# Two layers' split weights and four token operands laid out with steps of 2, 4 or 8 elements

## The chip, the cores and the metric

The kernel runs on one core of one Trainium2 chip. It is one program with five engines: TensorE multiplies (in the profile PE, and PEld for its weight loads), VectorE (DVE) and ScalarE (ACT) do elementwise work, GpSimd (POOL) and SyncE (SP) mostly issue transfers. Each engine works through its own queue in order and waits for the others by semaphores. The metric is the time of one execution on the device in microseconds; lower is better.

## The reference

Two layers over 512 tokens of width 1024, all in float32. Layer 0 mixes by dilated window attention, layer 1 by an mLSTM, and each is followed by a SwiGLU feed-forward of hidden width 2816:

```python
def swiglu(xn, w_in, w_out):
    gu = xn @ w_in
    return (jax.nn.silu(gu[..., :D_FF]) * gu[..., D_FF:]) @ w_out

def reference(x, positions, ...):
    h = x
    for i in range(DEPTH):
        j = i // N_MIXERS
        if i % N_MIXERS == 0:
            h = h + dilated_attention_mixer(rms_norm(h, attn_norm[j]), positions,
                                            attn_w_in[j], attn_w_out[j])
        else:
            h = h + mlstm_mixer(rms_norm(h, mlstm_norm[j]), mlstm_w_in[j], ...)
        h = h + swiglu(rms_norm(h, ffn_norm[i]), ffn_w_in[i], ffn_w_out[i])
    return rms_norm(h, final_norm)
```

## The kernel before

*Three matmuls for one.* TensorE multiplies the reduced type fp32r. To keep the precision of float32, every operand is split: ScalarE copies it into an fp32r tile (the high part, L239), VectorE subtracts that from the original into a second one (the low part, L241). A product is then the sum of high times high, high times low and low times high (`SPLITS`, three matmuls into one PSUM tile). A *chunk* is a tile of 128 partitions by 1024 elements of a weight matrix: four blocks of 128 rows (k) by 256 columns. A matmul takes as its weights 128 of those columns (k and a half m of the chunk), loads them into TensorE (PEld) and streams the token operand past them. Which operand lies where is told in elements: `weights_tiles` gives each chunk its high and its low tile, from pools of three buffers, at an offset inside the tile (`PAD`, and the pairs `WIDE`, `NARROW`, `TOKENS`); inside, the 1024 elements lie next to each other.

*Projections.* `project` and the plain part of the feed-forward (`plain`) multiply such chunks with all 512 tokens (`multiply`, L276: matmuls of 512 columns, 24 for each chunk). The names of the chunks say the matrix: awo (attention output), mqk, mo, mwo (the mLSTM's projections and its output), f0j0 to f1j2 (the first two pairs of hidden blocks of each feed-forward).

*Products.* The rest of the feed-forward's first matrix is done in blocks of 256 hidden columns, gate and up together (j = 4, 6, ... 20: nine blocks in each layer), by Winograd's form of Strassen's scheme: seven products of halves in place of eight. `PRODUCTS` lists them with their order: A11 x B11, S1 x T1, S2 x T2, A12 x B21, S3 x T3, S4 x B22, A22 x T4. A stands for chunks of weights, S for their sums and differences, which VectorE makes (`total`), B and T for quarters of the normalized tokens and their sums and differences, split once per layer by `split_tokens` into high and low tiles of 128 x 4 x 256. A product is 24 matmuls of 256 columns (`product`, L1680; 2 m, 4 k, 3 splits). `prepare` splits the weights of the product that comes two places later (`AHEAD` = 2), so that the splits run beside the products:

```python
            def prepare(key):
                made[key] = split(key)
                ...
        for n, (j, i) in enumerate(todo):
            some(1)
            prepare(n + AHEAD)
            ...
            steps_of[i]()
```

On VectorE a block then has seven low parts, four sums of weights, four rows that evacuate PSUM into the hidden tile, and in layer 1 also transposes of the residual (hB, L2363) that are stored by GpSimd's queue. On ScalarE it has seven high parts and five evacuations. The order on all engines is that of the program's text, as a scheduler of the framework lays it out; the waits come from which tile is read and written.

*Token operands.* `split_tokens` makes the high part with ScalarE (L1539) and the low part either with VectorE (L1544) or, for B11, T1 and T4, by a negated copy and an adding transfer. `T2`, `B21`, `T3` and `B22` go by VectorE. In layer 1, as in layer 0, that happens during the last plain chunks and the first products.

Of the kernel before, what the change touches and what calls it, by code (L numbers as in the profile page):

```python
# [11 lines left out]
F32 = mybir.dt.float32  # L12
F32R = mybir.dt.float32r
I32 = mybir.dt.int32
AF = mybir.ActivationFunctionType
ALU = mybir.AluOpType
AX = mybir.AxisListType
P = 128
# [58 lines left out]
def tile_hybrid_dilated_attn_mlstm(  # L77
# [5 lines left out]
    x = x[0]  # L83
# [138 lines left out]
    def run_late(_):  # L222
        while lows:
            with tc.issue_after(last_on(mybir.EngineType.DVE)):
                lows.pop(0)()

    def weights_tiles(name, at=WIDE):
        return [wp.tile([P, 1024 + PAD], F32R, tag="w" + x, name=name + "_" + x[0], bufs=W_BUFS)[:, o:o + 1024]
                for x, o in zip(("hi", "lo"), at)]

    def split_chunk(chunk, at=WIDE):

        raw, n, view, name = chunk
        if spare and next(splits) % (W_BUFS + 1) == W_BUFS:
            hi, lo = [spare[0].tile([P, 1024], F32R, tag="w%s4" % x, name=name + "_" + x[0]) for x in ("hi", "lo")]
        else:
            hi, lo = weights_tiles(name, at)
        with behind_factors():
            nc.scalar.activation(hi[:, :n], raw[:, :n], AF.Copy)  # L239
        def low():  # L240
            nc.vector.tensor_tensor(lo[:, :n], raw[:, :n], hi[:, :n].bitcast(F32), op=ALU.subtract)  # L241
        if late[0]:
            lows.append(low)
        else:
            with behind_scores():
                low()
        return view(hi), view(lo)
# [53 lines left out]
    class Feed:  # L301

        def __init__(self, ready, plan, ahead=2):
            self.ready, self.plan, self.ahead = ready, plan, ahead
# [1202 lines left out]
    def ffn_in(layer, fp, pair, rbc, hook, following, hid, during):  # L1507
# [21 lines left out]
        def op_tile(i, name):  # L1529
            return fp.tile([P, 4, HALF], F32R, tag="op%d" % i, name="f%d%s" % (layer, name))  # L1530


        ops, raw = {}, {}

        def split_tokens(key, by_dma=False):

            i = [b for _, b in PRODUCTS].index(key)
            hi, lo = ops[key] = [op_tile(2 * i + part, key + "hl"[part]) for part in range(2)]
            nc.scalar.activation(hi, raw[key], AF.Copy)  # L1539
            if by_dma:  # L1540
                nc.scalar.activation(lo, hi.bitcast(F32), AF.Copy, scale=-1.0)
                nc.gpsimd.dma_start(lo, raw[key], accum_op=ALU.add)
            else:
                nc.vector.tensor_tensor(lo, raw[key], hi.bitcast(F32), op=ALU.subtract)  # L1544
# [1032 lines left out]
```

## Time and profile before

| | us |
|---|---|
| two runs | 1348.9 and 1350.14 |
| median | 1349.52 |
| the profiled execution, by the clock of the device | 1350.34 |
| its span in the profile, first to last instruction | 1348.6 |

The span is 1.7 us shorter than the time of its own execution, which holds what lies before and after the program. The profile's page gives, by engine, the busy time with its share of the span; the row of forty slices (each digit the busy tenths of a slice of 33.7 us) shows whether that share is spread evenly:

```profile
PE   9999999999999999999999999999999999999997
DVE  7988789799876399888888899898858988997887
ACT  6676577667674255555577464795534555558855
PEclk9999999999999999999999999999999999999999
DMA  9354244555676357334362743324343535447863
```

TensorE is busy from end to end but for the last slice, at the full clock. The products of layer 0 lie between 521.7 and 693.4 us, those of layer 1 between 1062.3 and 1234.0 us, nine blocks of 19.04 us each.

### The profile page before, as it was taken

The page shows a single profiled execution, that of the slowest core. Times are in us where ns is not written, and L with a number is a line of the kernel's source. Part 1 is how long each engine was busy: PE and PEld are TensorE (multiplying, and loading weights), DVE is VectorE, ACT ScalarE, POOL GpSimd, SP SyncE. Part 2 cuts the span into 40 slices and gives each one's busy share as a digit, 9 for nine tenths or more (in the row PEclk, how much of TensorE's full clock was granted, in tenths as well). Part 3 has the DMA queues.
Part 4 walks back from the last instruction along what each step waited for, and adds up shares of the span by engine and source line. Part 5 has one row for each costly group of instructions (what it writes and reads, how often), then busy time and mean ns, then how long its engine had stood idle before and what let it go on. Part 6 is the DMA issues. An engine that isn't in the chain of part 4 may idle for free. (4 is left out here: it accounts for less than half of the span.)

```text
span 1348.6 us, 23346 instructions
## 1 busy us (share of the span) xinstructions
PE 1329.1 (99%) x9100; PEld 1219.9 (90%) x9100; DVE 1131.8 (84%) x1787; ACT 812.8 (60%) x1303; POOL 196.6 (15%) x272
## 2 busy tenths in 40 slices
PE   9999999999999999999999999999999999999997
PEld 7898899999998889999999998898888999999886
DVE  7988789799876399888888899898858988997887
ACT  6676577667674255555577464795534555558855
POOL 3000013141412001000010110122200202112113
PEclk9999999999999999999999999999999999999999
DMA  9354244555676357334362743324343535447863
GB/s 302 129 180 155 80 141 149 164 175 154 185 267 192 128 148 175 107 123 126 125 157 79 172 129 89 100 64 125 95 121 98 130 128 173 141 139 172 190 172 102
DMA packets 141270, 194.90 MB, mean 145 GB/s; under 512 B 9028, under 2 KB 106116, under 8 KB 141160
## 3 DMA queue, kind: packets, MB, share of 16 engines
q1 hardware_dynamic: 120128, 140.73, 33.3%
q0 software_dynamic: 19808, 52.48, 16.1%
q8 instruction: 71, 1.16, 0.4%
q10 hardware_dynamic: 1224, 0.21, 0.1%
q14 instruction: 39, 0.32, 0.1%
HBM read 167.30 MB, written 22.54 MB: 141 GB/s over the span
## 5 line engine op out<-in xcount | busy, mean ns | idle before, releaser
L1803 POOL DMA_DIRECT2D f0S<-in_ffn_w_out_dram x10 | 8.7, 875 | 245.0 <-DVE f0hid L1719 161.8
L2366 POOL DMA_DIRECT2D hD<-hB x32 | 20.7, 654 | 109.4 <-DVE hB L2363 109.2
L1827 POOL DMA_DIRECT2D f1T<-in_ffn_w_out_dram x15 | 17.8, 1186 | 86.1 <-ACT f1T L1830 40.5
L276 PE MATMUL mo<-n_h,mo_k_h 128*128 128x512 f32 x64 | 25.4, 397 | 0.0
L276 PE MATMUL mo<-n_h,mo_k_l 128*128 128x512 f32 x64 | 25.2, 394 | 0.0
L276 PE MATMUL awo<-ao_h,awo_k_h 128*128 128x512 f32 x64 | 25.2, 393 | 0.0
L276 PE MATMUL mo<-n_l,mo_k_h 128*128 128x512 f32 x64 | 25.1, 393 | 0.0
L276 PE MATMUL mwo<-yo_l,mwo_k_h 128*128 128x512 f32 x64 | 25.1, 392 | 0.0
L276 PE MATMUL mqk<-n_h,mqk_k_h 128*128 128x512 f32 x64 | 25.1, 392 | 0.0
L276 PE MATMUL mwo<-yo_h,mwo_k_l 128*128 128x512 f32 x64 | 25.1, 392 | 0.0
L276 PE MATMUL mqk<-n_l,mqk_k_h 128*128 128x512 f32 x64 | 25.1, 392 | 0.0
L276 PE MATMUL f0j<-n_h,f0j_h 128*128 128x512 f32 x64 | 25.0, 391 | 0.0
L276 PE MATMUL f1j<-n_h,f1j_h 128*128 128x512 f32 x64 | 25.0, 391 | 0.0
L276 PE MATMUL mwo<-yo_h,mwo_k_h 128*128 128x512 f32 x64 | 25.0, 391 | 0.0
L276 PE MATMUL mqk<-n_h,mqk_k_l 128*128 128x512 f32 x64 | 25.0, 391 | 0.0
L276 PE MATMUL awo<-ao_h,awo_k_l 128*128 128x512 f32 x64 | 25.0, 391 | 0.0
L276 PE MATMUL awo<-ao_l,awo_k_h 128*128 128x512 f32 x64 | 25.0, 390 | 0.0
L276 PE MATMUL f0j<-n_h,f0j_l 128*128 128x512 f32 x64 | 24.9, 390 | 0.0
L276 PE MATMUL f1j<-n_h,f1j_l 128*128 128x512 f32 x64 | 24.9, 390 | 0.0
L276 PE MATMUL f0j<-n_l,f0j_h 128*128 128x512 f32 x64 | 24.9, 389 | 0.0
L276 PE MATMUL f1j<-n_l,f1j_h 128*128 128x512 f32 x64 | 24.9, 389 | 0.0
L241 DVE TENSOR_TENSOR v1P_l<-v1W,v1P_h 128x1024 fp32r<-128x1024 f32 x14 | 17.1, 1223 | 9.2 <-ACT v1P_h L239 9.1
(2746 smaller groups left out, 5993.4 us busy)
## 6 DMA issues: line engine op xcount, KB each, us to landing
f0j_w<-in_ffn_w_in_dram SPq DMA_DIRECT2D x17, 512.0 KB, 6.0
f1j_w<-in_ffn_w_in_dram SPq DMA_DIRECT2D x17, 512.0 KB, 6.6
f1T<-in_ffn_w_out_dram POOLq DMA_DIRECT2D x15, 512.0 KB, 7.4
f0hid<-in_ffn_w_in_dram SPq DMA_DIRECT2D x9, 512.0 KB, 5.1
f1hid<-in_ffn_w_in_dram SPq DMA_DIRECT2D x9, 512.0 KB, 5.1
v0W<-in_attn_w_in_dram SPq DMA_DIRECT2D x8, 512.0 KB, 8.2
v1W<-in_attn_w_in_dram SPq DMA_DIRECT2D x8, 512.0 KB, 4.3
awo_k_w<-in_attn_w_out_dram SPq DMA_DIRECT2D x8, 512.0 KB, 4.0
```

What stands on the lines that cost most here:

```text
L241: nc.vector.tensor_tensor(lo[:, :n], raw[:, :n], hi[:, :n].bitcast(F32), op=ALU.subtract)
L276: nc.tensor.matmul(acc, whl[a][:, k, m * P:(m + 1) * P], pairs[b][kk], start=(kk == 0 and (a, b) == SPLITS[0]), stop=(kk == nk - 1 and (a, ...
L1803: nc.gpsimd.dma_start(t, src[1][:, ks], accum_op=ALU.add)
L1827: nc.gpsimd.dma_start(view(to), weight_rows(hk * UNITS + u, n), accum_op=ALU.add)
L2366: nc.gpsimd.dma_start(hD[k // 4].rearrange("(b i) x -> i b x", i=R)[:, :, c0:c0 + R], t[R * a_:R * (a_ + 1)])
```

## The change

The split weights and some token operands are laid out so that the elements that one matmul reads lie 2, 4 or 8 elements apart.

- *Wide chunks.* 42 chunks, in the order of `wide_names`: awo3 (2), f0j0, f0j2, f1j0, f1j2 (4 each), mqk0 to mqk3, mo0 to mo3, mwo0 to mwo3 (2 each). `WIDE_STEPS` has a place for each: step 2 for awo3, f0j0, f0j2 and f1j0, step 4 for f1j2, the eight mqk chunks and both of mo0, step 8 for the others; the tile's offset goes through 0, 8, ... 48, the low part's is the same or 8 more.
- *Chunks of the products.* All 126 (nine blocks, seven products, two layers) take a step by their j: step 2 for j = 4, 10, 14; step 4 for j = 6, 16, 20; step 8 for j = 8, 12, 18.
- *How a chunk is laid out.* With step 2 the two halves m of a row block k are interleaved column by column, with step 4 four of the (k, m) are, with step 8 all eight. `Stepped` gives back 128 columns with that step as a matmul's weights. ScalarE and VectorE write the high and the low part with the step (VectorE reads the high part with it too); with step 4 each does so in two instructions of 512 elements, otherwise in one of 1024.
- *Token operands of layer 1.* T2 and B22 are laid out with step 2 and B21 and T3 with step 4; B11, T1 and T4, and all of layer 0, stay as they were. T2 and B22 are split in four pieces of 256 columns on each of the two engines, B21 and T3 in one.
- Chunks split by `split_stepped` don't go through the branches of `split_chunk` for a spare buffer, for late low parts and behind the factors.

No matmul, transfer or sum is added or left out, and the matmuls come in the same order.

```diff
@@ -224,6 +224,43 @@
             with tc.issue_after(last_on(mybir.EngineType.DVE)):
                 lows.pop(0)()
 
+    WIDE_STEPS = [(s, (o, o + d)) for s in (2, 4, 8) for d in (0, 8) for o in range(0, 56, 7 * 8 // 7)]
+    wide_names = (["awo%d_k%d" % (c, k) for k in range(2) for c in range(3, 4)] +
+                  ["f%dj%d_%d%d" % (f, j, a, k) for f in range(2) for j in (0, 2) for k in range(2) for a in range(2)] +
+                  ["m%s%d_k%d" % (x, c, k) for x in ("qk", "o", "wo") for c in range(4) for k in range(2)])
+    NARROW_STEPS = [(2, (16, 48)), (4, (16, 48)), (8, (16, 48)), (2, (0, 0)), (8, (0, 0)), (2, (16, 16)), (4, (16, 16)),
+                    (8, (16, 16)), (4, (0, 32))]
+
+    class Stepped:
+
+        def __init__(self, t, k, step):
+            form = {2: "p (k c m) -> p k m c", 4: "p (k c l m) -> p k l m c", 8: "p (c k m) -> p k m c"}[step]
+            sizes = {2: dict(k=k, m=2), 4: dict(l=2, m=2, c=P), 8: dict(k=k, m=2)}[step]
+            self.step, self.ap = step, t.rearrange(form, **sizes)
+
+        def __getitem__(self, at):
+            _, k, cs = at
+            m = cs.start // P
+            return self.ap[:, k // 2, k % 2, m] if self.step == 4 else self.ap[:, k, m]
+
+        def like(self, t):
+            if self.step == 4:
+                return t.rearrange("p (k l m c) -> p k l m c", l=2, m=2, c=P)
+            return t.rearrange("p (k m c) -> p k m c", m=2, c=P)
+
+    def split_stepped(raw, name, step, at):
+        hi, lo = (Stepped(t, 4, step) for t in weights_tiles(name, at))
+        view = hi.like(raw)
+        parts = [(slice(None), i) for i in range(2)] if step == 4 else [(slice(None),)]
+        for part in parts:
+            nc.scalar.activation(hi.ap[part[0], part[1]] if step == 4 else hi.ap,
+                                 view[part[0], part[1]] if step == 4 else view, AF.Copy)
+        with behind_scores():
+            for part in parts:
+                h_, l_, r_ = (x[:, part[1]] if step == 4 else x for x in (hi.ap, lo.ap, view))
+                nc.vector.tensor_tensor(l_, r_, h_.bitcast(F32), op=ALU.subtract)
+        return hi, lo
+
     def weights_tiles(name, at=WIDE):
         return [wp.tile([P, 1024 + PAD], F32R, tag="w" + x, name=name + "_" + x[0], bufs=W_BUFS)[:, o:o + 1024]
                 for x, o in zip(("hi", "lo"), at)]
@@ -231,6 +268,11 @@
     def split_chunk(chunk, at=WIDE):
 
         raw, n, view, name = chunk
+        if name in wide_names:
+            return split_stepped(raw, name, *WIDE_STEPS[wide_names.index(name) % len(WIDE_STEPS)])
+        if at is NARROW and name[0] == "f" and name[1:3] in ("0j", "1j"):
+            j = int("".join(c for c in name[3:5] if c.isdigit()))
+            return split_stepped(raw, name, *NARROW_STEPS[(j - 4) // 2])
         if spare and next(splits) % (W_BUFS + 1) == W_BUFS:
             hi, lo = [spare[0].tile([P, 1024], F32R, tag="w%s4" % x, name=name + "_" + x[0]) for x in ("hi", "lo")]
         else:
@@ -1532,10 +1574,29 @@
 
         ops, raw = {}, {}
 
+        class Turned:
+
+            def __init__(self, t):
+                self.t = t
+
+            def __getitem__(self, at):
+                return self.t[:, at[1] // 2, at[1] % 2]
+
         def split_tokens(key, by_dma=False):
 
             i = [b for _, b in PRODUCTS].index(key)
             hi, lo = ops[key] = [op_tile(2 * i + part, key + "hl"[part]) for part in range(2)]
+            step = {"T2": 2, "B21": 4, "T3": 4, "B22": 2}.get(key) if layer else None
+            if step:
+                hi, lo = ops[key] = [t.rearrange("p k n -> p (k n)").rearrange(
+                    "p (k n l) -> p k l n" if step == 2 else "p (k n l) -> p (k l) n", k=4 // step, l=step) for t in (hi, lo)]
+                if step == 2:
+                    for k in range(4):
+                        nc.scalar.activation(hi[:, k // 2, k % 2], raw[key][:, k], AF.Copy)
+                        nc.vector.tensor_tensor(lo[:, k // 2, k % 2], raw[key][:, k], hi[:, k // 2, k % 2].bitcast(F32),
+                                                op=ALU.subtract)
+                    ops[key] = [Turned(t) for t in (hi, lo)]
+                    return
             nc.scalar.activation(hi, raw[key], AF.Copy)
             if by_dma:
                 nc.scalar.activation(lo, hi.bitcast(F32), AF.Copy, scale=-1.0)
```

Two places show what it does to the order. The first is VectorE's queue in layer 1 where the weights of block j = 6 are split beside the products of j = 4 (names with A, or hid and w, are chunks and the places where they were loaded, S the sums, h and l high and low). Before:

```order
L241 TENSOR_TENSOR f1j6A_l<-f1hid_11556,f1j6A_h 128x1024
L1686 TENSOR_TENSOR f1j4g_11594<-f1j_p_11434,f1j4u_11489 128x512
L241 TENSOR_TENSOR f1j6S_l<-f1j6S,f1j6S_h 128x1024
L1719 TENSOR_TENSOR f1hid_11593<-f1j4v_11459,f1j4g_11594 128x2x256
L1651 TENSOR_TENSOR f1j6S<-f1j6S,f1hid_11556 128x1024
```

After:

```order
L261 TENSOR_TENSOR f1j6A_l<-f1hid_11638,f1j6A_h 128x4x128 x2
L1747 TENSOR_TENSOR f1j4g_11678<-f1j_p_11516,f1j4u_11571 128x512
L261 TENSOR_TENSOR f1j6S_l<-f1j6S,f1j6S_h 128x4x128 x2
L1780 TENSOR_TENSOR f1hid_11677<-f1j4v_11541,f1j4g_11678 128x2x256
L1712 TENSOR_TENSOR f1j6S<-f1j6S,f1hid_11638 128x1024
```

Each low part has become two instructions of half the size at the same place; the evacuations (j4g, hid) and the sums stand where they stood. The second place is ScalarE's queue where layer 1's tokens are split, at the end of its plain chunks (f1j_01 and f1j_11). Before:

```order
L1539 ACTIVATE f1B22h<-f1x_11166 128x1024
L1539 ACTIVATE f1B21h<-f1x_11166 128x1024
L239 ACTIVATE f1j_11_h<-f1j_11_w 128x1024
L1539 ACTIVATE f1T1h<-f1t_11317 128x1024
L1539 ACTIVATE f1T3h<-f1x_11165 128x1024
L1541 ACTIVATE f1T1l<-f1T1h 128x1024
L1539 ACTIVATE f1T2h<-f1x_11166 128x1024
```

After:

```order
L1595 ACTIVATE f1B22h<-f1x_11228 128x256
L256 ACTIVATE f1j_01_h<-f1j_01_w 128x4x128 x2
L1595 ACTIVATE f1B22h<-f1x_11228 128x256 x3
L1600 ACTIVATE f1B21h<-f1x_11228 128x4x256
L256 ACTIVATE f1j_11_h<-f1j_11_w 128x4x128 x2
L1600 ACTIVATE f1T1h<-f1t_11387 128x1024
L1600 ACTIVATE f1T3h<-f1x_11227 128x4x256
L1602 ACTIVATE f1T1l<-f1T1h 128x1024
L256 ACTIVATE f1j4A_h<-f1hid_11451 128x4x2x128
L1595 ACTIVATE f1T2h<-f1x_11228 128x256 x4
```

T2 and B22 have come apart into four pieces each, one chunk's high part (f1j_01) now stands after the first piece of B22 instead of ahead of it, and one of block j = 4 stands ahead of T2 instead of behind it.

## The prediction

> **What bounds the kernel now.** I read the page first (busy times), then the chain that ended last, then the stage table of the second feed-forward, then single rows.
>
> ```profile
> PE 1329.1 (99%) x9100; PEld 1219.9 (90%) x9100; DVE 1131.8 (84%) x1787; ACT 812.8 (60%) x1303; POOL 196.6 (15%) x272
> 1081.83 2.72 PE f1j_c L1680 x24
> 1084.55 2.72 PE f1j_p L1680 x24
> ```
>
> The first line is the page's list of busy times, the other two are pieces of the chain. TensorE has almost no gap, and in the products the chain is one product after the other: 24 matmuls of 256 columns in 2.72 us, 113.3 ns each. Seven products make one block of hidden columns (one j): 168 matmuls, 19.04 us. The stage table, with a row for such a block in each layer (after the window and its length: PE, PEld, DVE, ACT, POOL busy, clock, DMA share, GB/s), shows how near the next engine is:
>
> ```profile
> 579.20:598.24 19.04, 19.04 (x170) 19.04 (x169) 16.30 (x17) 9.91 (x12) 0.00 (x0) 1.00 0.36 112
> 1138.79:1157.83 19.04, 19.04 (x170) 19.04 (x169) 17.36 (x19) 9.91 (x12) 4.81 (x8) 1.00 0.56 173
> 1028.00:1062.00 34.00, 34.00 (x151) 28.13 (x151) 29.17 (x39) 18.52 (x20) 2.21 (x2) 1.00 0.59 148
> 815.00:860.00 45.00, 45.00 (x248) 38.76 (x247) 42.54 (x80) 26.52 (x34) 1.66 (x2) 1.00 0.33 94
> ```
>
> VectorE has 2.7 us to spare in a block of layer 0 and 1.7 us in one of layer 1; ScalarE has 9. The clock is full. The weight loads are near their limit too. Where a matmul has only 128 columns, the load sets the pace, and the last output block shows it (start, length):
>
> ```profile
> 1339.84 0.19 PEld L2535 LDWEIGHTS finlast<-f1P_4w_h,f1P 128*128 128x128 f32 x1
> 1339.95 0.19 PEld L2535 LDWEIGHTS finlast<-f1P_4w_l,f1P 128*128 128x128 f32 x1
> 516.90 0.39 PE L276 MATMUL f0j<-n_h,f0j_h 128*128 128x512 f32 x1
> 517.12 0.39 PE L276 MATMUL f0j<-n_l,f0j_h 128*128 128x512 f32 x1
> ```
>
> So a dense load of 128 columns takes 0.11 us. A matmul of 512 columns gives it 0.227 us (the lower rows), one of 256 columns 0.113 us: 3 ns to spare.
>
> **The change part by part.** No matmul, transfer or sum is added; what moves is the address step inside the split weights and four token operands. That touches four readers or writers: VectorE's low parts, ScalarE's high parts, TensorE's weight loads, TensorE's streamed tokens. The trace of before has one store with a step of four elements and two such reads, against rows of the same work without a step:
>
> ```profile
> L2012 DVE TENSOR_TENSOR hn<-fo,h x8: 1098/1124/1153, 782.0 to 803.3; 128x512 f32<-128x512 f32 x8
> L1430 DVE TENSOR_TENSOR hn<-mwo,hn x8: 683/690/692, 983.8 to 1017.6; 128x512 f32<-128x512 f32 x8
> L455 DVE CAST angles<-posi x4: 261/270/289, 2.8 to 3.7; 1x128 f32<-1x128 int32 x4
> L463 DVE SCALAR_TENSOR_TENSOR angles<-angles x3: 291/291/293, 6.7 to 7.4; 128x128 f32<-128x128 f32 x3
> L833 DVE TENSOR_TENSOR a1ex<-a1xps,cst x1: 283/283/283, 277.0 to 277.0; 128x128 f32<-128x128 f32 x1
> ```
>
> The store at L2012 writes every fourth element and takes 1124 ns where the dense one takes 690: 434 ns more on 512 elements, 0.85 ns each. The reads at L455 (SBUF) and L833 (PSUM) step by four and cost no more than the dense 128 at L463. Stores with a step are dear, then; reads are not, at VectorE's pace of about one element per ns.
>
> *Low parts on VectorE* (126 in the products, 42 elsewhere). The dense rows, with ScalarE's, and two of the waits of one block from the timeline:
>
> ```profile
> L241 DVE TENSOR_TENSOR f1j_l<-f1j_w,f1j_h 128x1024 fp32r<-128x1024 f32 x8 | 9.8, 1222 | 1.4 <-ACT f1j_h L239 1.2
> L239 ACT ACTIVATE f1j_h<-f1j_w 128x1024 fp32r<-128x1024 f32 x8 | 8.4, 1054 | 10.4 <-PE f1j L276 9.3 <-PE mwo L276 1.1
> 1131.81 1.23 DVE L241 TENSOR_TENSOR f1j10A_l<-f1j10A,f1j10A_h 128x1024 fp32r<-128x1024 f32 x1 [0.34 <-ACT f1j10A_h L239]
> 1134.53 1.22 DVE L241 TENSOR_TENSOR f1j12A_l<-f1hid,f1j12A_h 128x1024 fp32r<-128x1024 f32 x1 [0.29 <-ACT f1j12A_h L239]
> 1137.25 1.22 DVE L241 TENSOR_TENSOR f1j12S_l<-f1j12S,f1j12S_h 128x1024 fp32r<-128x1024 f32 x1 [0.29 <-ACT f1j12S_h L239]
> ```
>
> Step 8: 1222 + 2 x 434 = 2090, 868 more. Step 4 is two halves of 512: 2 x 1124 = 2248, 1026 more. Step 2 has no row; between 0 and 868 I take 0, since the dense row is nearer to two neighbours in 16 bytes than to none. Of the nine blocks three have step 2, three step 4, three step 8. A step-4 block adds 7 x 1.03 = 7.2 us to VectorE, a step-8 block 7 x 0.87 = 6.1. In layer 0 that is 16.3 + 7.2 = 23.5 and 22.4 against TensorE's 19.04: over by 4.5 and 3.4, in sum 3 x 4.5 + 3 x 3.4 = 23.7 us. The lows run only two products ahead (three buffers), so little of that can be saved up in the step-2 blocks.
>
> *High parts on ScalarE.* No row of ScalarE stores with such a step: between nothing and VectorE's 0.85 ns an element, 0.87 us a chunk. Its sum even then is 9.9 + 6.1 = 16.0 of 19.04, so it is no bound. But VectorE's queue waits for it ahead of three of the seven lows (the rows above), and the later sums and evacuations stand behind. At the high end 3 x 0.87 = 2.6 us a block, 12 blocks, 31 us; at the low end 0. I take half, 16 us.
>
> *Token operands of layer 1.* T2 and B22 stream with step 2, B21 and T3 with step 4: 48 matmuls of each kind in a block, 432 in all. The dense stream takes 0.44 ns an element. VectorE's dense pace is (1222 - 690) / 512 = 1.04 ns an element, and the stepped reads of L455 and L833 fall behind it by nothing, so 256 stepped elements take at most 256 x 1.04 = 266 ns instead of 113, if TensorE reads them no worse than VectorE. Between 1 and 2.35 times I take twice for step 4, near the upper end, since TensorE would have to read more than twice as fast as any stepped read in the trace to lose nothing, and once for step 2, as with the low parts. Cost: 432 x 113.3 = 49.0 us, the ends 0 and 66. In these blocks TensorE then needs 19.04 + 5.44 = 24.5 us, and VectorE 17.36 + 7.2 = 24.6: VectorE's extra time in layer 1 is covered, to 0.1 us a block.
>
> *Weight loads.* Step 4 and 8 read 128 elements in 110 ns, 0.86 ns each, nearly the pace at which L455 and L833 show no penalty. I take 0; the other end is twice 110 (a rival below). Where matmuls have 512 columns even 220 hides under 227.
>
> *Plain chunks and token splits.* Eight mqk chunks add 8.2 us to VectorE where it has 2.5 us to spare in 45; not all of its work there is waited for: 4 us. Ahead of the layer-1 products four step-4 chunks and four token splits add 6.7 us to a window with 4.8 to spare: 2 us. The mo, mwo, awo and step-2 chunks meet a VectorE with room. In sum 6 us, between 0 and 10.
>
> Sum against the profiled execution, 1350.34 us (span 1348.6, 0.8 us above the median of 1349.52): 23.7 + 16 + 49.0 + 6 = 94.7, so **1445 us**.
>
> [...]
>
> **Rivals.**
> - A, *the weight load becomes the bound.* Stepped loads at half pace take 220 ns; it decides from 113 ns on. In 12 blocks 2016 matmuls go from 113.3 to 220: 215 us. The tokens then add only in the three step-2 blocks, 3 x 48 x 113.3 ns = 16 us, and 2 us in the others (227 over 220); VectorE is covered; plus 6: 1350 + 239 = 1589 us. For it: 3 ns of margin. Against it: the free stepped reads.
> - B, *the tokens stream free.* VectorE then bounds both layers: 23.7, and in layer 1 3 x 5.5 + 3 x 4.4 = 29.7, plus 16 and 6: 1426 us.
> - C, *tokens go by lines.* If a 16-byte line costs the stream what four dense elements cost (1.77 ns), step 2 is twice, step 4 four times: 9 x (48 x 113.3 + 48 x 340) ns = 196 us in layer 1, plus 23.7, 8 and 6: 1584 us. With A on top it passes 1700.
> - D, *not slower.* The 434 ns of L2012 are then a matter of its PSUM source read beside the dense one, not of the step, and a stepped low stays under 1222 + 2700 / 7 = 1600 ns: VectorE's spare time holds it, tokens and loads run free: 1350 us. If the step even took the 3 ns of margin out of the products (113.3 to 110 for 3024 matmuls), 10 us went: 1340. Against it: same shape, same operation, 690 with a PSUM source too (L1430).
>
> **How the numbers follow.** My forecast 0.37, A 0.29, B 0.15, C 0.07, D 0.12. The forecast's own range is 1405 (no ScalarE share, tokens at 1.8) to 1480. The range on record reaches from B's low side (half of the ScalarE share gone, 1395) to A with a little above: 1395 to 1605; it leaves out D and the combination beyond A, under 2 in 10. Two per cent, 27 us, is about what a measurement of this kernel tells from no change: below 1322.5 faster 0.03, within 0.09 (D), above 1376.5 slower 0.88.
>
> **What the changed profile would show.** Low parts of 2.1 us at step 8 and twice 1.12 at step 4, 1.22 at step 2; high parts of 1.1 (or 1.9) us; PE waiting for low parts in layer 0's step-4 and step-8 blocks. Layer 1's products on B21 and T3 at 5.4 us, on T2 and B22 at 2.72. Starts of stepped weight loads 0.113 us apart as before: 0.22 is rival A. I am wrong if lows stay under 1.6 us, if loads slow down, or if step 2 already costs.

## The result, and the profile after

The changed kernel takes 1679.55 us (two runs, 1678.90 and 1680.19) against 1349.52: 1.2445 times as long, 95% interval 1.2392 to 1.2499. The forecast was 1445, its range 1395 to 1605. The direction was right, the size was not. The profiled execution has a span of 1677.1 us.

The page's list of busy times after the change:

```profile
PE 1640.6 (98%) x9100; PEld 1552.0 (93%) x9100; DVE 1241.6 (74%) x1849; ACT 939.0 (56%) x1365; POOL 195.2 (12%) x272
```

TensorE is still busy from end to end, with the same 9100 matmuls, 311.5 us more of it. So in the main it does not wait for VectorE's parts, as the forecast had it: its own instructions became slower. Where, the table of stages tells (window and its length, then PE, PEld, DVE, ACT, POOL busy, clock, DMA share, GB/s); layer 0's products, the stretch between the two layers' products, and layer 1's products, before:

```profile
521.66:693.45 171.79, 171.79 (x1514) 171.55 (x1513) 150.00 (x152) 97.17 (x122) 3.90 (x4) 1.00 0.43 129
693.45:1062.30 368.85, 367.19 (x2236) 324.29 (x2235) 311.18 (x618) 218.55 (x388) 45.78 (x64) 1.00 0.43 113
1062.30:1233.99 171.69, 171.69 (x1513) 171.50 (x1512) 154.36 (x160) 96.58 (x122) 30.61 (x44) 1.00 0.47 143
```

and after:

```profile
522.34:822.78 300.44, 300.44 (x1514) 300.44 (x1512) 190.03 (x172) 143.43 (x143) 5.67 (x6) 1.00 0.26 77
822.78:1225.95 403.17, 386.38 (x2235) 368.23 (x2235) 336.64 (x634) 248.31 (x404) 43.27 (x62) 0.98 0.38 99
1225.95:1562.95 337.00, 334.27 (x1513) 329.47 (x1512) 199.15 (x185) 146.79 (x148) 30.91 (x45) 0.99 0.26 77
```

The 328.5 us of span are 128.7 in layer 0's products, 34.3 between, 165.3 in layer 1's, and 0.2 in the rest. In layer 0's products PE stays filled and the weight loads (PEld) are busy all the time. In the stretch between, PE has 16.8 us of gaps where it had 1.7, and the granted clock averages 0.98 where it was 1.00: in four spells, 17.1 us together, it stood at 0.5. One of these spells, and the starts of the matmuls of a wide chunk inside it and behind it:

```profile
1053.90:1057.30 3.40, 3.40 (x10) 2.69 (x10) 3.13 (x5) 1.05 (x7) 0.00 (x0) 0.50 0.11 41
...
1055.04 0.63 PE L318 MATMUL mo<-n_l,mo_k_h 128*128 128x512 f32 x1
1055.47 0.63 PE L318 MATMUL mo<-n_h,mo_k_l 128*128 128x512 f32 x1
...
1057.48 0.40 PE L318 MATMUL mo<-n_l,mo_k_h 128*128 128x512 f32 x1
1057.72 0.40 PE L318 MATMUL mo<-n_h,mo_k_l 128*128 128x512 f32 x1
```

The starts are 0.43 us apart inside the spell and 0.24 us behind it. PE was busy in 15.5 us of the four spells, so half the clock cost some 8 us (an estimate). The loss in the stretch is thus in large part of another kind than the one in the products.

Single blocks of the products after the change: j = 4 (step 2), 6 (step 4) and 8 (step 8) of layer 0, then j = 8 (step 8) and 10 (step 2) of layer 1:

```profile
522.34:542.50 20.16, 20.16 (x170) 20.16 (x168) 19.42 (x21) 14.29 (x16) 3.92 (x4) 1.00 0.83 192
542.50:582.07 39.57, 39.57 (x171) 39.57 (x169) 25.01 (x24) 17.34 (x17) 0.00 (x0) 1.00 0.20 62
582.07:622.59 40.52, 40.52 (x169) 40.52 (x169) 21.49 (x17) 15.35 (x12) 0.00 (x0) 1.00 0.17 52
1299.67:1340.33 40.66, 40.66 (x169) 40.66 (x169) 21.48 (x17) 15.37 (x12) 2.57 (x4) 1.00 0.19 58
1340.33:1371.30 30.97, 30.97 (x170) 29.35 (x169) 15.15 (x14) 12.51 (x12) 4.74 (x8) 1.00 0.35 111
```

A block of 168 matmuls took 19.04 us (the first of each layer 19.47 and 19.37). Now it takes 20.16 with step 2, 39.57 with step 4 and 40.52 with step 8: 120, 236 and 241 ns a matmul. VectorE's 25.01 us fit inside 39.57 with room. Layer 1's token operands show only in the step-2 block (30.97 against 20.16); with step 8 they add 0.14 us. The single rows of the timeline (start, length) show who sets the pace. Weight loads of layer 0 with step 2 (j = 4), step 4 (j = 6) and step 8 (j = 8), then in layer 1's block j = 10 the matmuls on B11 (dense), T2 (step 2) and B21 (step 4):

```profile
530.02 0.19 PEld L1741 LDWEIGHTS f0j_u<-f0T2h,f0j4S_l 128*128 128x128 f32 x1
530.14 0.20 PEld L1741 LDWEIGHTS f0j_u<-f0T2h,f0j4S_h 128*128 128x128 f32 x1
...
559.32 0.33 PEld L1741 LDWEIGHTS f0j_c<-f0B21h,f0j6A_h 128*128 128x128 f32 x1
559.55 0.33 PEld L1741 LDWEIGHTS f0j_c<-f0B21l,f0j6A_h 128*128 128x128 f32 x1
...
609.92 0.34 PEld L1741 LDWEIGHTS f0j_u<-f0T3h,f0j8S_l 128*128 128x128 f32 x1
610.16 0.34 PEld L1741 LDWEIGHTS f0j_u<-f0T3h,f0j8S_h 128*128 128x128 f32 x1
```

```profile
1341.89 0.28 PE L1741 MATMUL f1j_c<-f1B11l,f1j10A_h 128*128 128x256 f32 x1
1342.01 0.29 PE L1741 MATMUL f1j_c<-f1B11h,f1j10A_l 128*128 128x256 f32 x1
...
1349.75 0.42 PE L1741 MATMUL f1j_u<-f1T2l,f1j10S_h 128*128 128x256 f32 x1
1349.98 0.41 PE L1741 MATMUL f1j_u<-f1T2h,f1j10S_l 128*128 128x256 f32 x1
...
1354.87 0.43 PE L1741 MATMUL f1j_c<-f1B21h,f1j10A_l 128*128 128x256 f32 x1
1355.10 0.43 PE L1741 MATMUL f1j_c<-f1B21h,f1j10A_h 128*128 128x256 f32 x1
```

Read the distance of the starts: the loads come every 0.12, 0.23 to 0.24 and 0.24 us, the matmuls every 0.12 us on a dense operand and every 0.23 us on a stepped one, whether its step is 2 or 4. The elementwise engines' own rows, by groups (minimum, median and maximum in ns): low parts on VectorE with step 2, with step 8 and with step 4 (in halves), then high parts on ScalarE likewise:

```profile
L261 DVE TENSOR_TENSOR f0j_l<-f0j_w,f0j_h x8: 1221/1226/1228, 469.3 to 508.3; 128x1024 fp32r<-128x1024 f32 x8
L261 DVE TENSOR_TENSOR mwo_k_l<-mwo_k_w,mwo_k_h x8: 2097/2244/2334, 1115.4 to 1164.0; 128x1024 fp32r<-128x1024 f32 x8
L261 DVE TENSOR_TENSOR f0j6S_l<-f0j6S,f0j6S_h x4: 1093/1108/1122, 540.9 to 547.1; 128x512 fp32r<-128x512 f32 x4
...
L256 ACT ACTIVATE f0j_h<-f0j_w x8: 1117/1136/1182, 466.1 to 506.3; 128x1024 fp32r<-128x1024 f32 x8
L256 ACT ACTIVATE mwo_k_h<-mwo_k_w x8: 2076/2268/2314, 1113.1 to 1161.8; 128x1024 fp32r<-128x1024 f32 x8
L256 ACT ACTIVATE f0j6S_h<-f0j6S x4: 1138/1160/1176, 539.7 to 545.8; 128x512 fp32r<-128x512 f32 x4
```

(The mwo rows are step 8, f0j6S step 4 in halves, f0j step 2.) The forecast's prices for VectorE (1.22, twice 1.12 and 2.09 us) hold within 7%: 1.23, twice 1.11, 2.24 us. ScalarE's parts with steps 4 and 8 have more than doubled, twice 1.16 or 2.27 where a dense one took 1.05.

### The profile page after: what moved, and what is told of

Read it like the earlier page. It is cut to its first block, busy times and chain, and to the rows that moved or that the text cites. A ratio compares the mean times of both kernels' runs of the same rounds, so it can differ in the third digit from the quotient of the medians.

```text
span 1677.1 us, 23467 instructions
## 1 busy us (share of the span) xinstructions
PE 1640.6 (98%) x9100; PEld 1552.0 (93%) x9100; DVE 1241.6 (74%) x1849; ACT 939.0 (56%) x1365; POOL 195.2 (12%) x272
## 3 DMA queue, kind: packets, MB, share of 16 engines
q8 instruction: 71, 1.16, 0.3%
## 5 line engine op out<-in xcount | busy, mean ns | idle before, releaser
L261 DVE TENSOR_TENSOR mwo_k_l<-mwo_k_w,mwo_k_h 128x1024 fp32r<-128x1024 f32 x8 | 17.9, 2234 | 9.9 <-ACT mwo_k_h L256 9.8
L318 PE MATMUL awo<-ao_h,awo_k_l 128*128 128x512 f32 x64 | 25.1, 392 | 0.0
```

The source lines that it names most:

```text
L261: nc.vector.tensor_tensor(l_, r_, h_.bitcast(F32), op=ALU.subtract)
L318: nc.tensor.matmul(acc, whl[a][:, k, m * P:(m + 1) * P], pairs[b][kk], start=(kk == 0 and (a, b) == SPLITS[0]), stop=(kk == nk - 1 and (a, ...
```

## The experiments

The kernel of each experiment ran once with a profile, beside a run of the kernel before on the same chip (1349.5 to 1350.5 us). The table gives their times and, worked out from the starts of the matmuls, the length of three stages, in us. Three more kernels, map_steps, map_runs and map_offsets (1619.4, 1503.6 and 1364.6 us), change a pattern from block to block and are read block by block further down.

| kernel | time | layer 0's products | between | layer 1's products |
|---|---|---|---|---|
| before | 1349.5 | 171.8 | 368.9 | 171.7 |
| after | 1679.6 | 300.4 | 403.2 | 337.0 |
| tokens_dense | 1641.6 | 300.4 | 401.4 | 301.5 |
| weights_dense | 1453.8 | 171.8 | 369.1 | 275.9 |
| reads_only | 1618.1 | 300.4 | 377.5 | 300.4 |
| stores_only | 1440.3 | 196.8 | 402.6 | 202.3 |
| stores_dve | 1413.1 | 189.7 | 389.0 | 195.2 |
| stores_act | 1391.9 | 184.3 | 382.6 | 184.9 |
| wide_only | 1385.1 | 171.5 | 401.2 | 173.1 |
| all_step2 | 1372.8 | 181.2 | 371.7 | 181.3 |

**Tokens or weights.** Two runs take one of them back. tokens_dense:

```diff
-            step = {"T2": 2, "B21": 4, "T3": 4, "B22": 2}.get(key) if layer else None
+            step = None
```

> Only the weights keep their steps; layer 1's four token operands are dense again. Theory L (a weight load with step 4 or 8 takes about 240 ns where a dense one takes at most 113, and sets the pace): in the trace after the change only the three step-2 blocks of layer 1 are longer than those of layer 0 by the tokens (31.0 and 34.0 against 20.2 us), the others by 0.1 to 0.2; so layer 1 comes to layer 0's 300.4 us from 337.0 and the time to 1679.6 - 36.6 = 1643 us. Theory T (the tokens' steps are the main cost): four of seven products in all nine blocks come back to 2.72 us, 9 x 4 x 2.9 = 104 us less, 1576.

It took 1641.6 us, with layer 1's blocks like layer 0's (20.2, 39.6, 40.5) but for the first, which took 21.2. Theory L gave 1643. weights_dense:

```diff
-        if name in wide_names:
+        if False:
...
-        if at is NARROW and name[0] == "f" and name[1:3] in ("0j", "1j"):
+        if False:
```

> Only layer 1's token operands T2, B22 (step 2) and B21, T3 (step 4) keep their steps; all weights are dense. If step 2 costs a streamed token as much as step 4 (5.52 and 5.62 us for a product in the step-2 blocks after the change, where a dense one takes 2.72): 9 x (2 x 2.8 + 2 x 2.9) = 103 us, 1350 + 103 = 1453. If only step 4 costs, as the prediction had it: 9 x 48 x 113.3 ns = 49 us, 1399; the 5.52 us of T2 and B22 would then come from the weights' step 2 together with the tokens'.

It took 1453.8, as expected if step 2 costs the streamed operand as much as step 4. In a block of 30.39 us the three dense products take 2.72 to 2.81 us, those on T2 and B22 5.47 and 5.49, those on B21 and T3 5.59. Alone, the tokens cost 104 us; in the changed kernel only 35.5 of it shows (337.0 against 301.5 in tokens_dense), since a stepped weight load (236 ns) covers a stepped stream (230 ns).

**Reads or stores.** Two runs part what TensorE reads from what the other engines write. reads_only stores densely:

```diff
-        for part in parts:
-            nc.scalar.activation(hi.ap[part[0], part[1]] if step == 4 else hi.ap,
-                                 view[part[0], part[1]] if step == 4 else view, AF.Copy)
+        nc.scalar.activation(hi.flat, raw, AF.Copy)
...
+            nc.vector.tensor_tensor(lo.flat, raw, hi.flat.bitcast(F32), op=ALU.subtract)
```

> The reverse: ScalarE and VectorE store the parts densely, in one instruction each, and only TensorE reads its weights with the steps of the change (so the columns are permuted and the products are not the reference's); all tokens are dense. Theory L: the loads alone make the time, 1643 us as with dense tokens, products at 5.65 us with step 4 and 5.79 with step 8. If the stores' traffic has a share in the slow loads: below 1600, with loads well under 236 ns apart.

stores_only lets TensorE read densely:

```diff
-            return self.ap[:, k // 2, k % 2, m] if self.step == 4 else self.ap[:, k, m]
+            return self.flat[:, (2 * k + m) * P:(2 * k + m + 1) * P]
```

> ScalarE and VectorE store the high and low parts with the steps of the change, but TensorE reads 128 neighbouring elements of the tiles as weights (so the columns are permuted and the products are not the reference's), and all tokens are dense. This takes the slow loads away and leaves the prediction's VectorE term. VectorE had 22.6 us of work in a step-4 block of layer 0 and 24.0 in a step-8 block after the change, against 19.04 of TensorE's: 3 x 3.5 + 3 x 5 = 25 us a layer, 50 in both, some more in the projections: 1400 to 1430 if VectorE then bounds. If stores with a step were the whole cause by disturbing TensorE's reads: near 1643, with weight loads still 236 ns apart. If they are hidden: 1350 to 1360.

With the reads alone layer 0's products are as slow as with the whole change, to a tenth of a us in each block (300.4 us in both), and layer 1's blocks are the same again: here the loads owe nothing to the stores' traffic. The total is 1618 and not 1643, because the stretch between the products came back to 377.5, without waits and at the full clock. The expectation had left that stretch out. What is left there, 8.6 us, are the slow loads of the wide chunks: their matmuls of 512 columns start 0.236 us apart for mqk (step 4) and 0.246 us for mwo (step 8), where they started 0.227 us apart. With the stores alone the stretch is 402.6, with both 403.2, so the two do not add there. The time with the stores alone is 1440, 10 us above the expected 1400 to 1430. TensorE now has gaps in the products too. What ended them in layer 0, and in the stretch between (waiting and line, what it waited for, us, times, longest):

```profile
PE f0j_u L1741 <- ACT f0j_u L1753: 9.1, 6, 2.6
PE f0j_u L1741 <- DVE f0j12S_l L261: 1.3, 1, 1.3
...
PE m1nb L2293 <- ACT m0e L2303: 4.1, 1, 4.1
...
PE m6yT L414 <- DVE m6yt L2348: 2.3, 1, 2.3
```

The longest wait of the products is not for a low part. It is for ScalarE's copy of the first product into the bank of the third (f0j_u, L1753), which stands in ScalarE's queue behind two high parts of 2.1 to 2.2 us. VectorE has a share in it: in block j = 8 the first of the two had stood 3.22 us for a sum that VectorE made after a low part of 2.14 us. Between the products TensorE waits for the chain of layer 1's mixer (the m rows). reads_only has none of these waits left (0.3 us, one wait), the kernel before had 1.3 us.

**ScalarE or VectorE.** Two runs keep the steps on one of the two engines, with dense reads. stores_dve and stores_act:

```diff
-            nc.scalar.activation(hi.ap[part[0], part[1]] if step == 4 else hi.ap,
-                                 view[part[0], part[1]] if step == 4 else view, AF.Copy)
+            at_ = slice(part[1] * 512, part[1] * 512 + 512) if step == 4 else slice(0, 1024)
+            nc.scalar.activation(hi.flat[:, at_], raw[:, at_], AF.Copy)
```

```diff
-                nc.vector.tensor_tensor(l_, r_, h_.bitcast(F32), op=ALU.subtract)
+                at_ = slice(part[1] * 512, part[1] * 512 + 512) if step == 4 else slice(0, 1024)
+                nc.vector.tensor_tensor(lo.flat[:, at_], raw[:, at_], hi.flat[:, at_].bitcast(F32), op=ALU.subtract)
```

> As the run with the change's stores alone (dense reads by TensorE, dense tokens), but ScalarE's high parts are stored densely and only VectorE's low parts with the steps (the parts then don't belong to each other, so the products are not the reference's). That run took 90 us more than before: 25 in layer 0's products, 34 between the products, 31 in layer 1's. Theory V (VectorE's time is the cost there): nearly all of it stays, 1420 to 1440. Theory Q (low parts come late because the high parts before them are late): half or less stays, under 1400.

> The other half: only ScalarE's high parts are stored with the steps, VectorE's low parts densely (again the parts don't belong to each other). A high part took 1.15 us for 512 elements and 2.15 to 2.27 for 1024 with a step of 4 or 8, against 1.05 for 1024 dense. The prediction put ScalarE's share at 16 us, between 0 and 31. Theory V: under 20 us, 1350 to 1370. Theory Q: 1390 to 1420.

(In stores_act the low part is the original minus what lies at the same place of the high tile, so the two still add up to the weights; that remark of the expectation was mistaken.) Theory V missed both times. Theory Q missed for VectorE (1413, not under 1400), and its 1390 to 1420 held for ScalarE (1392). VectorE alone costs 63 us, ScalarE alone 42, both 90. If 5.5 us in each layer's products are put down to the offsets (below) in each of the three runs, the two add: 12.4 + 7.0 = 19.4 against 19.5 for both in layer 0, 18.0 + 7.7 = 25.7 against 25.1 in layer 1, 20.1 + 13.7 = 33.8 against 33.7 between. That the offsets cost their full price in each run is not shown. In stores_dve the blocks with step 4 and 8 are as long as VectorE's work, as here in j = 8 of layer 0:

```profile
561.59:584.47 22.88, 19.95 (x171) 19.35 (x169) 22.65 (x18) 10.16 (x13) 0.00 (x0) 1.00 0.32 100
```

VectorE is busy in 22.65 of 22.88 us, and the offset of such a block may cost nothing. If only the two step-2 blocks at other offsets pay (1.12 and 0.75 us), VectorE's share in layer 0 is 16.1 us; so it lies between 12.4 and 16.1. The first rows of TensorE's waits in layer 0's products, of stores_dve and of stores_act:

```profile
PE f0j_u L1741 <- DVE f0j8S_l L261: 2.4, 2, 2.1
```

```profile
PE f0j_u L1742 <- ACT f0j_u L1754: 4.5, 3, 1.7
```

So each engine holds TensorE up mostly through its own queue: VectorE with late low parts, ScalarE with the late copy.

**The wide chunks alone.** wide_only has the products and the tokens as before:

```diff
-        if at is NARROW and name[0] == "f" and name[1:3] in ("0j", "1j"):
+        if False:
...
-            step = {"T2": 2, "B21": 4, "T3": 4, "B22": 2}.get(key) if layer else None
+            step = None
```

> Only the 42 wide chunks keep their steps; the products' weights and all tokens are as before. The stretch between the two layers' products went from 368.9 to 403.2 us with the change, 402.6 with the change's stores and dense reads, and 377.5 with its reads and dense stores. If the chunks' stores in the queues of ScalarE and VectorE delay the recurrence of layer 1's mixer, which TensorE waits for, this is 1350 + 34 + 1 = 1385 us, with TensorE's waits for the m rows (18 us with the change) as they were. The prediction's term for these chunks was 6 us: 1356.

1385.1 us, as expected to the us, with the m rows' waits as in the changed kernel. The expectation had taken the stretch as it was measured after the change, so the agreement shows that the wide chunks make it, but not by which path. Of the 32.3 us more, 15.4 are gaps of PE, and three spells at half the clock, 10.2 us together, cost about 5 (an estimate, half of the 10.2); slower loads, 8.6 us in reads_only, make most of the rest. VectorE's timeline in this run shows one of the waits:

```profile
983.35 2.38 DVE L261 TENSOR_TENSOR mwo_k_l<-mwo_k_w,mwo_k_h 128x1024 fp32r<-128x1024 f32 x1 [1.06 <-ACT mwo_k_h L256]
985.57 0.17 DVE L196 SCALAR_TENSOR_TENSOR m6rq_a<-m6rq_y 128x4 f32<-128x4 f32 x1
...
987.56 1.13 DVE L2348 TENSOR_SCALAR m6yt<-m6num,m6rr 128x128 f32<-128x128 f32 x4
```

VectorE stands 1.06 us for a late high part, then takes 2.38 us for the low part. Ten tiny steps of the mixer (m6rq, m6rr) stand behind it in the queue, and m6yt, for which TensorE waits 2.1 us, comes after them.

**Which steps are slow.** map_steps is the kernel before with dense stores; only the address pattern that TensorE reads in the products differs from block to block (step, run of neighbours, first element):

```diff
+WEIGHT_MAP = {4: (1, 1, 0), 6: (2, 1, 0), 8: (3, 1, 0), 10: (4, 1, 0), 12: (5, 1, 0), 14: (6, 1, 0), 16: (7, 1, 0), 18: (8, 1, 0), 20: (2, 1, 1)}
+TOKEN_MAP = {4: (2, 1, 0), 6: (3, 1, 0), 8: (4, 1, 0), 10: (4, 2, 0), 12: (4, 2, 1), 14: (4, 2, 2), 16: (8, 4, 0), 18: (8, 4, 2), 20: (2, 1, 1)}
...
+                    whl = [Pattern(x.rearrange("p k n -> p (k n)"), *pattern) for x in whl]
...
+                moving = Pattern(ops[okey][b].rearrange("p k n -> p (k n)"), *tokens).cut(HALF)
```

> The kernel before, with every part stored densely, but in the products TensorE reads by a step that differs from block to block (so the products are not the reference's). Layer 0, weights: j = 4 to 18 read with step 1, 2, 3, 4, 5, 6, 7, 8, j = 20 step 2 from the second element. Layer 1, tokens: j = 4, 6, 8 step 2, 3, 4; j = 10 pairs of neighbours every four elements, from element 0 of the four; j = 12 the same from element 1; j = 14 from element 2; j = 16 four neighbours every eight; j = 18 the same from element 2; j = 20 step 2 from element 1. Theory G (a load's time goes by how many groups of four elements, 16 bytes, it touches: 236 ns for 128 groups at step 4): 113 at step 1 and 119 at step 2 (64 groups), 96 groups at step 3, so 177 ns, and 236 to 242 from step 4 to 8. Theory S (any step over 2 is slow): 236 at step 3 as well. Tokens: steps 2 and 4 both took about 230 ns, so not by such groups (64 or 128 of them to 256 columns would differ by half). Theory N (two neighbours come in one read, 0.9 ns each read): 113 for pairs and for fours that lie on even elements (j = 10, 14, 16, 18), 230 for steps 2, 3, 4 (j = 4, 6, 8, 20); pairs from element 1 (j = 12) 230 if the two must lie in the same 8 bytes, else 113. Blocks of 168 matmuls: 19.0 us at 113 ns, 38.6 at 230.

The blocks' lengths say it directly. Weights with step 2, 3 and 4, then tokens as pairs every four, fours every eight, and fours every eight from element 2:

```profile
540.64:560.80 20.16, 20.16 (x170) 20.16 (x169) 16.56 (x17) 9.90 (x12) 0.00 (x0) 1.00 0.45 140
560.80:590.30 29.50, 29.50 (x171) 29.50 (x169) 17.75 (x18) 9.88 (x12) 0.00 (x0) 1.00 0.23 72
590.30:629.86 39.56, 39.56 (x170) 39.56 (x169) 16.58 (x16) 9.88 (x12) 0.00 (x0) 1.00 0.18 54
...
1291.30:1329.78 38.48, 38.48 (x170) 34.93 (x169) 16.59 (x16) 9.88 (x12) 4.76 (x8) 1.00 0.28 89
1406.68:1426.49 19.81, 19.81 (x170) 19.81 (x168) 16.23 (x17) 9.89 (x12) 2.58 (x4) 1.00 0.35 110
1426.49:1464.93 38.44, 38.44 (x171) 34.91 (x169) 19.01 (x20) 9.89 (x12) 4.74 (x8) 1.00 0.30 94
```

By 168, a load takes 120, 176 and 236 ns; with steps 5 to 8 it was 227, 227, 234 and 242. Step 3 decides between the theories: 128 elements lie in 96 groups of 16 bytes, theory G gave 177, theory S 236. So a load that touches 64, 96 or 128 groups of four elements took 1.88, 1.83 and 1.77 to 1.89 ns for each. Below 64 groups this pace is not shown: a dense load touches 32 groups, which would be 59 ns, and the prediction's rows of finlast have such loads 0.11 us apart. For tokens theory N fell: pairs, on either half of a group, are as slow as single elements (229 ns); only fours on a group's boundary kept the pace (118).

map_runs asks whether the boundary counts once, where a run begins, or for each group:

```diff
+WEIGHT_MAP = {4: (1, 1, 1), 6: (1, 1, 2), 8: (3, 1, 1), 10: (4, 1, 1), 12: (4, 1, 3), 14: (5, 1, 1), 16: (6, 1, 2), 18: (7, 1, 3), 20: (2, 1, 3)}
+TOKEN_MAP = {4: (1, 1, 1), 6: (1, 1, 2), 8: (12, 8, 0), 10: (16, 8, 2), 12: (12, 4, 0), 14: (20, 16, 0), 16: (24, 16, 2), 18: (132, 128, 0), 20: (8, 4, 1)}
```

> As the first map of steps, with other patterns (the products are not the reference's). Layer 1, tokens by block: j = 4 dense from element 1, j = 6 dense from element 2, j = 8 eight neighbours every 12, j = 10 eight from element 2 every 16, j = 12 four every 12, j = 14 sixteen every 20, j = 16 sixteen from element 2 every 24, j = 18 128 every 132, j = 20 four from element 1 every 8. In the first map only whole groups of four on a 16-byte boundary kept the pace (117 ns; pairs, and fours from element 2, 229). Theory W (a whole group of four is taken at once, any other element by itself at 0.9 ns): dense from element 1 or 2 near 113, eight from element 2 172 (half the elements in whole groups), sixteen from element 2 142. Theory B (where the runs begin decides for all): 229 for all of j = 4, 6, 10, 16, 20, and 113 to 117 for j = 8, 12, 14, 18. Layer 0, weights: j = 4, 6 dense from element 1, 2; then step 3 from 1, step 4 from 1 and from 3, step 5 from 1, step 6 from 2, step 7 from 3, step 2 from 3. By the number of groups touched the place of the first element changes nothing: 113 to 120, 175, 236, 236, 227, 227, 235, 119.

Its blocks of tokens in eights from element 2 every 16 and in sixteens from element 2 every 24 (the block dense from element 1 took 19.84 us):

```profile
1235.92:1263.93 28.01, 28.01 (x170) 28.01 (x169) 17.70 (x18) 9.88 (x12) 4.76 (x8) 1.00 0.38 124
1303.50:1328.70 25.20, 25.20 (x171) 25.20 (x169) 18.39 (x20) 9.87 (x12) 2.58 (x4) 1.00 0.31 96
```

Dense from element 1, in eights and in sixteens a matmul took 118, 167 and 150 ns, where theory W gave 113, 172 and 142 and theory B 229 for all three. The four blocks of runs on a boundary took 116 to 120, fours from element 1 230. Theory W is within 10 ns everywhere, with misses to both sides, and theory B is far off: by these blocks a whole group of four takes the time of two single elements (1.8 ns, 113 ns for 64 groups), each other element 0.9 ns by itself (230 ns for 256), to within that error. The weights were as expected within 2 ns, whatever the first element.

**Offsets, and step 2 everywhere.** The stores-only run had a by-product: dense reads, and still 120 and 118 ns in the blocks j = 10 and 14, whose tiles lie at other offsets than before. map_offsets and all_step2:

```diff
-                return split_chunk((w[key], 1024, lambda t: t.rearrange("p (k n) -> p k n", k=4), nm + key), NARROW)
+                return split_chunk((w[key], 1024, lambda t: t.rearrange("p (k n) -> p k n", k=4), nm + key), OFFSETS[j])
```

```diff
-    WIDE_STEPS = [(s, (o, o + d)) for s in (2, 4, 8) for d in (0, 8) for o in range(0, 56, 7 * 8 // 7)]
+    WIDE_STEPS = [(s, (o, o + d)) for s in (2, 2, 2) for d in (0, 8) for o in range(0, 56, 7 * 8 // 7)]
...
-    NARROW_STEPS = [(2, (16, 48)), (4, (16, 48)), (8, (16, 48)), (2, (0, 0)), (8, (0, 0)), (2, (16, 16)), (4, (16, 16)),
-                    (8, (16, 16)), (4, (0, 32))]
+    NARROW_STEPS = [(2, (16, 48)), (2, (16, 48)), (2, (16, 48)), (2, (0, 0)), (2, (0, 0)), (2, (16, 16)), (2, (16, 16)),
+                    (2, (16, 16)), (2, (0, 32))]
```

> The kernel before, stored densely, but the weight tiles of the products lie at other offsets (high, low) by block: j = 4 (16, 48) as before, then (0, 0), (16, 16), (0, 32), (0, 16), (0, 8), (0, 4), (32, 48), (0, 64). In layer 0 TensorE reads them densely, in layer 1 with step 2 (there the products are not the reference's). With dense reads the run with the change's stores alone had 113 ns at (16, 48) and 118 to 120 ns at (0, 0), (16, 16) and (0, 32). Theory O (offsets alone cost up to 7 ns, whatever the step): dense 113 at (16, 48), 118 to 121 at the three others, and step 2 the same as dense at each offset but for (16, 48), where it has 119. Theory X (the 118 to 120 ns came from the stores with steps beside the loads): dense 113 at all offsets here.

> All of the change's weights with step 2 and its offsets, the tokens dense. Loads of 119 to 121 ns instead of 113.3 make a block 20.16 us instead of 19.04: 18 x 1.12 = 20 us; the 42 wide chunks at 5.56 instead of 5.44 us 5 us; VectorE's low parts stay at 1.22 us and stall nothing: 1350 + 25 = 1375. If steps over 2 owe their time to the interleaved layout as such (order of the columns, ScalarE's and VectorE's views) and not to the distance, this too is far above 1400.

Dense blocks took 19.3 us at (16, 48), the first of the layer, and 20.16, 19.79, 20.01, 19.81, 19.88, 19.79, 19.41 and 20.15 at the other offsets in the order of the expectation; step 2 took 19.8 to 20.2 at every offset. The block at (0, 0):

```profile
539.57:559.73 20.16, 20.16 (x171) 20.16 (x169) 16.57 (x17) 9.88 (x12) 0.00 (x0) 1.00 0.45 140
```

Theory X falls. Of theory O the main point holds: the offset alone can cost 2 to 7 ns a matmul, the step of 2 costs 7 at the one offset that was free, and the two don't add at (0, 0), where both have 120 ns. That step 2 is the same as dense at each other offset does not hold: at (32, 48) dense reads took 116 ns and step 2 took 120. By these blocks the change's offsets cost 2 x 1.12 + 3 x 0.75 + 0.97 = 5.5 us a layer where reads are dense and nothing else sets the pace. With step 2 in all weights and dense tokens the map costs 23 us (1372.8 against the expected 1375): the interleaving as such is nearly free, and what is dear begins past step 2, where a load took 120 ns: 176 at step 3, where 128 elements lie in 96 groups, and 236 at step 4, where each has its own.

## Why the prediction was wrong, step by step

- **Weight loads: the step that failed.** "I take 0; the other end is twice 110." They take twice and a little more, 233 to 242 ns, in twelve blocks: with the 3 us of the step-2 blocks 128.7 us a layer by the table's first stage, nearly four fifths of the loss. The two rows that spoke for 0 were VectorE's. L833 (283 ns) read PSUM, another memory than the weights'. L455 took 270 ns for 128 elements, on another engine; what VectorE loses there does not tell what TensorE's load loses (236 ns at step 4). Nor do these rows show that VectorE lost nothing. L463, with which L455 was compared, reads two operands; dense rows of 128 elements with one operand took 217 to 226 ns (L458, L461, L464) and 301 (L457) in the same trace, so 270 ns for L455 decides nothing. "Where matmuls have 512 columns even 220 hides under 227" fell with it: the loads take more than 227 (matmuls 236 and 246 ns apart with steps 4 and 8), and reads_only has 8.6 us for that between the products. With 3 ns of margin, the argument would have had to be near certain to be worth taking.
- **Rival A was the right mechanism at 1589.** What separates it from 1680: 12 blocks at 40.0 us on average instead of 37.0, 36 us; the six step-2 blocks at 20.16, 7; layer 1's products 36.6 over layer 0's, for the tokens, instead of 18, 19; the stretch between 34 instead of 6, 28. Together 90 us, and 1589 + 90 = 1679. Its half pace was the author's estimate. In map_steps a load takes 120 ns at step 2, 176 at step 3 and 236 at step 4; streamed tokens lose half already at step 2 (229 ns a matmul against 113).
- **Low parts on VectorE.** Each one's price was right within 7%, and stores_dve shows VectorE as the bound that the forecast meant. The term, 23.7 us in layer 0, was too large: alone it is 12.4 to 16.1. VectorE's busy time there rose from 150.0 to 183.4 us, by 33.4 where the forecast's prices add up to 39.9. In the changed kernel it is nothing, since the block grew to 39.6 us around VectorE's 25. The forecast had looked for TensorE's waits at these parts; the trace after has them nowhere in layer 0.
- **High parts on ScalarE.** The upper end (VectorE's extra) was too low: 1.0 to 1.3 us a chunk more instead of 0.87. The share of 8 us a layer came out near the measured 7.0 and 7.7, which is luck, since the way was another: not through the low parts, but through the copy (f0j_u), which TensorE waits for directly. In the changed kernel it too is covered.
- **Tokens.** Twice for step 4 was right (5.59 against 2.72 us). Its "once for step 2" was not: 5.5 us. Alone 104 us instead of 49; with the slow loads 35.5, nearly all of it in the three step-2 blocks, as rival A's own working had it. Rival C had twice for step 2 right, and four times for step 4 wrong.
- **Plain chunks.** 6 us forecast, 34 measured, outside its bounds of 0 to 10. The step was to weigh VectorE's added work against its idle time in the window. The idle time was there, but the mixer's chain of short steps runs through the same two queues, and a long store that stands ahead of a link delays the chain. One such place is shown above (m6yT); most of the other waits also last about 2 us, as long as one stored part. The waits make 15.1 of the 34.3 us. Two more parts were in no term: some 8 us of half clock, and the slow loads of these chunks, 8.6 us in reads_only. The forecast treated mo and mwo as meeting "a VectorE with room".
- **The range** reached to 1605 for A "with a little above", and so took A's load at exactly twice the dense one and every other term at its forecast. It fell short by 75 us.

How the slow loads, the slow stream and the stores work together in the products is shown by the runs: the larger one set a product's time. With loads at 241 ns the stream at 230 ns added 0.14 us to a block (40.66 against 40.52), VectorE's 25.01 us lay inside a block of 39.57, and with dense reads its 22.65 filled one of 22.88 (stores_dve). Why groups of 16 bytes come out as the unit, why the offsets matter, and what sets off the spells at half the clock, was not tried.

## What to carry to other kernels

Lay weights so that the 128 columns of one load fall into 64 groups of 16 bytes or fewer (113 to 120 ns a load here, 176 with 96 groups, 227 to 242 with 128), and streamed operands in whole groups of four float32 on their boundary (113 to 120 ns a matmul, 229 to 233 for single elements); here, in matmuls of 256 columns, the first cost up to 2.1 times, the second 2.0 times (with 512 columns the slow loads cost 4 to 8%). A pace measured on one engine is no price for another's reads: where the nearest instruction has a margin of 3 ns, put the unknown price on the dear side and take the terms together at their upper ends for the range. Before a longer instruction is called hidden by an engine's idle time, look whose chain it stands ahead of in that engine's queue.

## What the runs showed of the hardware that was not expected

- A load with step 5 or 6 takes 227 ns, less than with step 4 (236) or 8 (242), though each touches 128 groups.
- A stream that starts off a group's boundary keeps nearly the whole pace if it is contiguous (118 and 122 ns from elements 1 and 2, against 113), but runs of four that straddle a boundary lose half (229).
- The place of a dense weight tile, by 16 bytes and more, moves a 256-column matmul from 113 ns to between 116 and 120; of the nine pairs of offsets that were tried (16, 48) alone was free.
- VectorE's store with step 2 costs nothing (1226 against 1222 ns), ScalarE's 8% (1136 against 1054).
- The granted clock fell to 0.5 for 3.41 us or twice that between the products of the changed kernel (four times, 17.1 us), with the stores alone (23.9 us) and with the wide chunks alone (10.2 us). The kernel before and reads_only, with 1.7 and 0.3 us of gaps in PE there, had none; stores_act had 11.5 us of gaps and none either, so gaps alone do not tell when it falls.
